# A loop over further token blocks, moved ahead of the experts behind eight weight loads

## The chip, the cores and the metric

The kernel runs on one core of a Trainium2 chip. The metric is the time on the device, in microseconds (us), of one execution; each kernel is run several times and the median is given. The core's engines run side by side and wait for each other by semaphores: PE is TensorE (matrix products and transposes through the identity), DVE is VectorE, ACT is ScalarE, POOL is GpSimd, and SP is SyncE, which here only issues the large loads. Each engine carries out its own instructions in a fixed order.

## The reference

Two model blocks, one after the other, over 1024 tokens of width 1024, in float32. The first has two token mixers and a feed-forward part; the second has two more mixers and a mixture of experts. Only the last is touched by the change:

```python
p_group = softmax(h @ wg + bg)            # 4 groups
pg, g_sel = top_k(p_group, 1)
e_in = (h @ we + be)[the 8 experts of g_sel]
top_v, top_i = top_k(e_in, 2)
gates = softmax(top_v) * pg
ids = g_sel * 8 + top_i                   # 2 of 32 experts for each token
hg = xs @ w_gate[e];  hu = xs @ w_up[e]   # [1024] -> [512], rows xs of expert e
y  = (silu(hg) * hu) @ w_down[e]          # [512] -> [1024]
out = rmsnorm(x + sum over both of gate * y)
```

A token goes to two experts, so 2048 rows are shared out over 32 experts. How many an expert gets depends on the data; the kernel has to be right for any share.

## The kernel before, in words

**Products.** Each float32 matrix is split into a high part (a copy on ScalarE, line 56, `split`) and a low part (source minus high, line 57), which together are one "unit" of 128 x 1024 elements. The low part is VectorE's; among the experts every sixth (`self.nsplit % 6 == 5`) is GpSimd's. A product (`mm3`, lines 87 to 89) is three matmuls: high by high, high by low, low by high. The pool of units holds five.

**Weights.** They arrive in pieces of 1 MB in a ring of 14 slots (`rawt`); SP issues the loads in program order, each as soon as its slot is free.

**Routing** (`route`). It makes for each expert the list of its rows: the first 128 of each expert come straight into a table on the chip (`self.sidx` and `self.slots`), and all of them are also written as records to a list in memory, `lst`, by eight indirect DMAs on GpSimd for each half of the tokens (`scatter`, line 1255). The scatter of the second half is kept as `self.scatter` and called among the experts, at `e == 2`.

**Experts** (`stage5`, from line 1269). For each of 32 experts one block of 128 rows is processed. `gather(e)` fetches the rows by an indirect DMA on GpSimd into one of two tiles xg (line 1298). `prep(e)` transposes them on TensorE; ScalarE and VectorE evict the result as xT (line 138). `wide` makes gate and up products (tile gu), 4 units each; a tanh on ScalarE (th, line 1357) and two VectorE operations make the hidden values; `hidT` transposes them (hT, line 138); `down` makes the product dn from 4 units. Its two halves are scaled by the gate while ScalarE evicts them as y (line 1338), and an indirect DMA scatters the rows to `yd` (line 1339). The loop is staggered by one: turn e makes the gate product of expert e, then the transposes of the hidden values of e−1, the up product of e, the transposes of the input of e+1, and the down product of e−1. A turn has 12 units, 72 matmul products of 512 columns and 12 transposes; two of its units have a low part by GpSimd.

**Further blocks** (`overflow`, from line 1387). For an expert with more than 128 rows a loop whose count is known only on the chip processes the remaining blocks. TensorE sums the counts (line 1396, `cnt`), VectorE makes from them a table of blocks (lines 1399 to 1417), each engine loads the number of blocks into a register (line 1418), and all five engines enter the loop at line 1420; its body reads `lst`. It is called at `e == NX // 2`, that is, behind 16 of 32 experts.

**Order.** The program is written in one stream, and a scheduler decides the order on each engine from its dependences and estimated times. It doesn't move instructions across the loop at line 1420. So what stands ahead of the loop, its body, and what stands behind it are ordered apart.

**End.** Behind the experts the two rows of each token are added, normed and written out (lines 1371 to 1385).

Of the kernel before, what the change touches and what calls it, by code (L numbers as in the profile page):

```python
# [8 lines left out]
F32 = mybir.dt.float32  # L9
# [7 lines left out]
P = 128  # L17
S = 1024
D = 1024
# [5 lines left out]
NX = NG * NE  # L25
DE = 512
BIG = 1 << 20
OFF = 4096
# [3 lines left out]
class Net:  # L32
# [27 lines left out]
    def t_units(self, w, cols):  # L60
        """Column tiles (128 wide) of w [K, N]; loaded in pairs where they adjoin."""
        nc = self.nc
        i = 0
        while i < len(cols):
            c = cols[i]
            n = 2 if i + 1 < len(cols) and cols[i + 1] == c + P else 1
            raw = self.raw_p.tile([P, KD, n * P], F32, tag="raw", name="raw")
            nc.sync.dma_start(raw, w[:, c:c + n * P].rearrange("(k p) c -> p k c", p=P))
            for j in range(n):
                yield self.split(raw[:, :, j * P:(j + 1) * P], [KD, P])  # L70
            i += n

    def n_units(self, w, r0, nk, c0):
        """Row tiles of w, 512 columns from c0, two row tiles a unit."""
        nc = self.nc
        for k in range(0, nk, 4):
            m = min(4, nk - k)
            raw = self.raw_p.tile([P, m, 512], F32, tag="raw", name="raw")
            nc.sync.dma_start(
                raw, w[r0 + k * P:r0 + (k + m) * P, c0:c0 + 512].rearrange("(k p) c -> p k c", p=P))  # L80
            for j in range(0, m, 2):
                yield k + j, self.split(raw[:, j:j + 2], [2, 512])

    def mm3(self, out, w, x, first, last):
        """out += w^T x, both as (high, low) pairs; w is the one held in the array."""
# [5 lines left out]
    def col(self, ps, unit, xT, n0=0, n=HT):  # L91
        """ps [128 columns, n tokens] = unit^T xT"""
# [7 lines left out]
    def pair(self, slot, name):  # L100
        """A (high, low) pair [128, 8, 512] in one of the two large slots."""
# [8 lines left out]
    def rstd(self, pool, ssq, n, scale=1.0):  # L110
        """(scale * ssq / n + eps) ^ -0.5 for [128, m]"""
        nc = self.nc
# [7 lines left out]
    def norm(self, pool, x, gB, out):  # L120
        """out = rmsnorm(x) * g for a natural tile [128, 1024]"""
# [7 lines left out]
    def to_T(self, psp, xn, dst, t0, nk=KD, k0=0, tag="tp"):  # L129
        """dst (high, low) [:, k, t0:t0+128] = xn[:, k*128:(k+1)*128]^T"""  # L130
# [10 lines left out]
    def rows_T(self, psp, wk, tmp, specs, name, tag="tp"):  # L141
        """Vectors of DRAM, as rows of 128, turned to columns: {name: [128, n] AP}."""
# [17 lines left out]
    def stage1(self):  # L160
        tc, nc, a = self.tc, self.nc, self.a
        self.x2d = self.dram.tile([S, D], F32, name="x2d")
        with ExitStack() as ctx:
# [56 lines left out]
            # softplus(-lambda)  # L220
# [6 lines left out]
            # block-diagonal maps of the heads 2c, 2c + 1 for c of a pair  # L227
# [12 lines left out]
            for hf in range(2):  # L240
                T0 = hf * HT

                # short convolution branch
# [42 lines left out]
                # recurrent branch  # L286
                yb = self.pair(1 - hf, "yb")
                for c in range(0, 8, 2):
# [25 lines left out]
                    def gates():  # L314
                        for j in range(2):
# [7 lines left out]
                            # x = -log a = 4 sp (1 + tr);  1 - a = (1 + e^-x) tanh(x / 2)  # L323
# [7 lines left out]
                        # sqrt(1 - a^2) = (1 + a) sqrt(tanh(x / 2))  # L331
# [36 lines left out]
                # the next transposed input is made while the last product runs  # L368
# [23 lines left out]
    def put(self, dst, k, src):  # L392
        """dst (high, low) [:, k] = src"""
# [4 lines left out]
    def softplus(self, tmp, out, x, sgn, bias=0.0):  # L398
        """out = log(1 + exp(y)), y = sgn * x + bias; tmp() gives a tile like out."""
# [5 lines left out]
        # log1p(e) = 2 atanh(z), z = e / (2 + e) <= 1/3  # L405
# [11 lines left out]
    def stage2(self):  # L417
        tc, nc, a = self.tc, self.nc, self.a
        with ExitStack() as ctx:
# [78 lines left out]
            # the last two pairs by halves, so that the next input is ready in time  # L498
# [18 lines left out]
    def stage4(self):  # L517
# [11 lines left out]
        with ExitStack() as ctx:  # L529
# [38 lines left out]
            # the router's norm weight goes into its matrix  # L568
# [5 lines left out]
            # rows 0..15: dt of the heads, 32..39: i, 64..71: f  # L574
# [42 lines left out]
            def half(hf, xT, box):  # L617

# [27 lines left out]
                # dt rows halved, since xs is held doubled  # L646
# [18 lines left out]
                # exponents: decay | wc;  exp(acs) | inter;  - | exp(-m)  # L665
# [20 lines left out]
                # natural columns: [token, chunk, (16 heads | 8 heads)]  # L686
# [16 lines left out]
                def conv_silu(u, cw, cb, halo, i, n, out):  # L703
                    """out = 2 silu(conv(x) + b) for channel tile i of n"""
# [132 lines left out]
                def out_row(yT, q, u):  # L837
                    """The product of one row tile of w_out, token tile by token tile."""
# [44 lines left out]
                def heads(p, R):  # L883
                    """The two heads of a pair, each in three parts: weights, chunks, result."""
# [31 lines left out]
                    def part_c(e):  # L916
# [23 lines left out]
                        # h = num / den, normed over its 128 channels  # L940
# [8 lines left out]
                        # the weights of the state are spent: their place takes the result  # L949
# [18 lines left out]
                def mix_M(p, R, late):  # L968
                    """Two heads; between their parts stands what is left of the two before."""
# [41 lines left out]
            for hf in range(2):  # L1011
# [7 lines left out]
                for kind, j, n in units:  # L1019
# [14 lines left out]
                    if hf and kind == "M" and j < 3:  # L1034
                        # the routing of the first half stands between the heads of the second
# [11 lines left out]
    def merge(ga, na, gb, nb):  # L1047
        """The steps of ga with nb steps of gb spread among them."""
# [8 lines left out]
    def weave(self, ga, na, gb, nb):  # L1057
        """Traces the steps of two generators in turn."""
# [19 lines left out]
    def route_const(self):  # L1078
# [8 lines left out]
        # descending ranks, for the first of equals  # L1087
# [18 lines left out]
    def route(self, hf, src, wk, small, wide, mx):  # L1106
        """Experts, gates and places of half the tokens, in steps; their records go to the experts' lists."""
# [4 lines left out]
        for tt in range(4):  # L1112
            x = src(tt)
            t = hf * 4 + tt
            # the logits come from x itself: its norm's scale follows, its weight is in the matrix
# [17 lines left out]
        # 0 .. 127 along the row; low[q, p] = 1 where q < p; ones  # L1133
# [22 lines left out]
        def first_max(x, n, top, one):  # L1156
            """top = max of x [P, 4, n], one = one-hot of its first place"""
# [27 lines left out]
        # gates: softmax of the two, times the group's probability; halved for the doubled silu  # L1185
# [13 lines left out]
        # places: those before in the tile, in the tiles before and in the half before  # L1199
# [12 lines left out]
        n = 0  # L1212
        qs = []
        for s, gt in ((0, pg), (1, m2)):
# [7 lines left out]
            # what a slot of an expert's first block holds: row of the result, token, gate;  # L1222
            # less OFF, so that slots without a token stand out of bounds
# [18 lines left out]
        for s, r, gt in ((0, r1, pg), (1, r2, m2)):  # L1242
            # row of the list = pos * 32 + 8 * group + expert, both as 4 - rank and 8 - rank
# [25 lines left out]
    def stage5(self):  # L1269
        tc, nc, a = self.tc, self.nc, self.a  # L1270
        self.wctx.close()
        with ExitStack() as ctx:
# [34 lines left out]

            def wide(w, e, xT):
                ps = psa.tile([P, DE], F32, tag="gu", name="gu", bufs=4)
                for k in range(0, KD, 4):  # L1310
                    raw = self.rawt([P, 4, DE])
                    nc.sync.dma_start(raw, w[e, k * P:(k + 4) * P, :].rearrange("(k p) c -> p k c", p=P))
# [12 lines left out]
            def down(e, hT):  # L1325
                pd = [psa.tile([P, 512], F32, tag="dn", name="dn") for _ in range(2)]
                for k in range(0, 4, 2):
                    raw = self.rawt([P, 2, D])
                    nc.sync.dma_start(raw, wd[e, k * P:(k + 2) * P, :].rearrange("(k p) c -> p k c", p=P))
# [16 lines left out]
            self.ysc = []  # L1346
            gather(0)
            gather(1)
            xT = prep(0)
            prev = None  # L1350
            for e in range(NX + 1):
# [14 lines left out]
                if e == 2:  # L1366
                    self.scatter()
                if e == NX // 2:
                    # the other tile of xg holds the next but one
                    self.overflow(mid, wk, psa, xg[(e + 1) % 2])  # L1370
# [16 lines left out]
    def overflow(self, mid, wk, psa, x):  # L1387
        """Blocks of 128 tokens past an expert's first, as many as there are."""
# [31 lines left out]
        with tc.For_i(0, nb) as i:  # L1420
            e = nc.sync.value_load(ti[0:1, bass.ds(i, 1)], min_val=0, max_val=NX - 1)
# [123 lines left out]
```

## Time and profile before

| | us |
|---|---|
| median of three runs | 3396.74 |
| the three runs | 3396.74, 3402.04, 3393.51 |
| the profiled execution, its span | 3397.5 |
| span less median | 0.8 |

| engine | busy us | share of the span |
|---|---|---|
| PE | 3230.0 | 95% |
| DVE | 2072.2 | 61% |
| ACT | 1419.9 | 42% |
| POOL | 609.1 | 18% |

The profile records one execution; the trace's zero is the start of the span. The experts begin at about 2716 us with the gather of the first rows and end at 3345.5; the 52 us behind that are the end of the kernel. A row of a timeline gives start, duration, engine, line, operation, output<-input, how many alike stand together, and in brackets the idle time of the engine before it and what released it. Neighbouring products overlap in the records: of two products that start 0.23 us apart each may show 0.40. [...]

### The profile page before, as it was taken

The numbers are of one execution on the slowest core, as the hardware profiler recorded it, in microseconds if no ns is written. First come the engines' busy times: TensorE is split into PE (matmuls) and PEld (weight loads), VectorE is DVE, ScalarE is ACT, GpSimd is POOL, SyncE is SP. The second block draws the span as 40 slices with busy tenths as digits, with TensorE's granted clock in tenths as the row PEclk, the third lists the DMA queues.
The fourth block names the chain that finished last, engine by engine and source line by source line (L and its number), as shares of the span: only waits on it lengthen the run. The fifth ranks groups of instructions, "written<-read, shape, count | busy, mean of one in ns | idle before, by whom it ended". The sixth has DMA issues, their size and how long they took to land. (4 is left out here: it accounts for less than half of the span.)

```text
span 3397.5 us, 39631 instructions
## 1 busy us (share of the span) xinstructions
PE 3230.0 (95%) x15457; PEld 2661.3 (78%) x15457; DVE 2072.2 (61%) x2869; ACT 1419.9 (42%) x1954; POOL 609.1 (18%) x649
## 2 busy tenths in 40 slices
PE   8999999999999999999999999899999899999993
PEld 6887888877778888888777888777888778878772
DVE  5437544365544334333787665877656678888886
ACT  3227432255321111111343333443443378878873
POOL 0002210011210000000232111132112143334433
PEclk9999999999999999999999999999999899999996
DMA  4332433323431111111323323243332699969993
GB/s 154 99 100 85 145 118 99 99 85 117 136 118 50 50 50 38 62 50 35 105 88 106 103 91 92 73 145 109 103 109 93 230 322 384 381 256 389 368 349 155
DMA packets 313080, 487.81 MB, mean 144 GB/s; under 512 B 28400, under 2 KB 190460, under 8 KB 311868
## 3 DMA queue, kind: packets, MB, share of 16 engines
q1 hardware_dynamic: 291532, 427.02, 36.5%
q0 software_dynamic: 19488, 51.44, 4.2%
q10 hardware_dynamic: 1872, 6.82, 0.5%
q8 instruction: 122, 2.00, 0.2%
q14 instruction: 66, 0.54, 0.0%
HBM read 465.65 MB, written 36.34 MB: 148 GB/s over the span
## 5 line engine op out<-in xcount | busy, mean ns | idle before, releaser
L57 DVE TENSOR_TENSOR unit<-raw,unit 128x1024 fp32r<-128x1024 f32 x682 | 887.0, 1321 | 434.1 <-ACT unit L56 427.1
L56 ACT ACTIVATE unit<-raw 128x1024 fp32r<-128x1024 f32 x746 | 775.8, 1057 | 770.7 <-PE acc L89 689.5
L87 PE MATMUL acc<-xT,unit 128*128 128x512 f32 x1712 | 679.3, 397 | 0.1
L88 PE MATMUL acc<-xT,unit 128*128 128x512 f32 x1712 | 672.2, 393 | 0.0
L89 PE MATMUL acc<-xT,unit 128*128 128x512 f32 x1712 | 670.3, 392 | 0.0
L87 PEld LDWEIGHTS acc<-xT,unit 128*128 128x128 f32 x1712 | 323.7, 189 | 68.7 <-issue 1.2
L88 PEld LDWEIGHTS acc<-xT,unit 128*128 128x128 f32 x1712 | 323.4, 189 | 68.4 <-issue 3.6
L89 PEld LDWEIGHTS acc<-xT,unit 128*128 128x128 f32 x1712 | 323.2, 189 | 68.2 <-issue 1.0
L88 PE MATMUL gu<-unit,xT 128*128 128x512 f32 x512 | 207.3, 405 | 16.7 <-POOL unit L57 9.5
L87 PE MATMUL gu<-unit,xT 128*128 128x512 f32 x512 | 207.2, 405 | 1.1 <-ACT xT L138 0.8
L89 PE MATMUL gu<-unit,xT 128*128 128x512 f32 x512 | 204.5, 400 | 0.0
L88 PE MATMUL acc<-unit,xT 128*128 128x256 f32 (+1 forms) x640 | 196.4, 307 | 2.0 <-DVE unit L57 2.0
L87 PE MATMUL acc<-unit,xT 128*128 128x256 f32 (+1 forms) x640 | 193.9, 308 | 3.1 <-ACT xb L709 3.0
L89 PE MATMUL acc<-unit,xT 128*128 128x256 f32 (+1 forms) x640 | 195.4, 306 | 0.0
L57 POOL TENSOR_TENSOR unit<-raw,unit 128x1024 fp32r<-128x1024 f32 x64 | 157.7, 2464 | 156.8 <-issue 89.9
L482 DVE SCALAR_TENSOR_TENSOR xh<-acc,xh 128x512 f32<-128x512 f32 x160 | 110.4, 690 | 85.1 <-PE acc L89 84.5
L87 PE MATMUL acc<-unit,hid 128*128 128x512 f32 x352 | 137.3, 390 | 0.0
L89 PE MATMUL acc<-unit,hid 128*128 128x512 f32 x352 | 137.2, 390 | 0.0
L87 PE MATMUL acc<-x2T,unit 128*128 128x512 f32 x352 | 137.1, 389 | 0.1
L88 PE MATMUL acc<-unit,hid 128*128 128x512 f32 x352 | 137.1, 389 | 0.0
L88 PE MATMUL acc<-x2T,unit 128*128 128x512 f32 x352 | 136.9, 389 | 0.0
L89 PE MATMUL acc<-x2T,unit 128*128 128x512 f32 x352 | 136.9, 389 | 0.0
(425 smaller groups left out, 5641.0 us busy)
## 6 DMA issues: line engine op xcount, KB each, us to landing
raw<-in_w_in_dram SPq DMA_DIRECT2D x104, 1024.0 KB
raw<-in_exp_w_gate_dram SPq DMA_DIRECT2D x64, 1024.0 KB
raw<-in_exp_w_up_dram SPq DMA_DIRECT2D x64, 1024.0 KB
raw<-in_exp_w_down_dram SPq DMA_DIRECT2D x64, 1024.0 KB
raw<-in_w_ffn_gate_dram SPq DMA_DIRECT2D x11, 1024.0 KB
raw<-in_w_ffn_up_dram SPq DMA_DIRECT2D x11, 1024.0 KB
raw<-in_w_ffn_down_dram SPq DMA_DIRECT2D x11, 1024.0 KB
raw<-in_w_out_dram SPq DMA_DIRECT2D x9, 1024.0 KB
```

What stands on the lines that cost most here:

```text
L56: nc.scalar.activation(h, src, AF.Copy)
L57: (low or nc.vector).tensor_tensor(l, src, h.bitcast(F32), ALU.subtract)
L87: mm(out, w[0], x[0], start=first, stop=False)
L88: mm(out, w[0], x[1], start=False, stop=False)
L89: mm(out, w[1], x[0], start=False, stop=last)
L482: nc.vector.scalar_tensor_tensor(xs, ps, 0.5, xs, op0=ALU.mult, op1=ALU.add)
```

## The change

Eight weight loads are issued first: gate and up of expert 0, gate of expert 1, down of expert 0. The gathers of experts 0 and 1 follow, then the loop over further blocks, and behind it all experts; the four lines that fetched a piece of weights inside `wide` and `down` first look among those loaded ahead. The call of the loop at `e == NX // 2` and that of `self.scatter()` at `e == 2` are gone. The scatter now stands inside the loop's body: it is carried out once for each turn of the loop, and not at all when there is none. The loop gets a tile of its own for its rows (`xo`), cleared in the body. Comments were removed as well; those lines are left out here.

```diff
+            ahead = {}
+            def wload(w, e, k):
+                raw = self.rawt([P, 4, DE])
+                nc.sync.dma_start(raw, w[e, k * P:(k + 4) * P, :].rearrange("(k p) c -> p k c", p=P))
+                return raw
+            def dload(e, k):
+                raw = self.rawt([P, 2, D])
+                nc.sync.dma_start(raw, wd[e, k * P:(k + 2) * P, :].rearrange("(k p) c -> p k c", p=P))
+                return raw
             def wide(w, e, xT):
                 ps = psa.tile([P, DE], F32, tag="gu", name="gu", bufs=4)
                 for k in range(0, KD, 4):
-                    raw = self.rawt([P, 4, DE])
-                    nc.sync.dma_start(raw, w[e, k * P:(k + 4) * P, :].rearrange("(k p) c -> p k c", p=P))
+                    raw = ahead.pop((w is wu, e, k), None)
+                    if raw is None:
+                        raw = wload(w, e, k)
...
                 for k in range(0, 4, 2):
-                    raw = self.rawt([P, 2, D])
-                    nc.sync.dma_start(raw, wd[e, k * P:(k + 2) * P, :].rearrange("(k p) c -> p k c", p=P))
+                    raw = ahead.pop((2, e, k), None)
+                    if raw is None:
+                        raw = dload(e, k)
...
             self.ysc = []
+            for key in ((0, 0, 0), (0, 0, 4), (1, 0, 0), (1, 0, 4), (0, 1, 0), (0, 1, 4), (2, 0, 0), (2, 0, 2)):
+                j, e, k = key
+                ahead[key] = dload(e, k) if j == 2 else wload((wg, wu)[j], e, k)
             gather(0)
             gather(1)
+            self.overflow(mid, wk, psa, mid.tile([P, D], F32, tag="gB", name="xo"))
+            self.nraw = len(ahead)
             xT = prep(0)
...
                 if e:
                     down(e - 1, hT)
-                if e == 2:
-                    self.scatter()
-                if e == NX // 2:
-                    self.overflow(mid, wk, psa, xg[(e + 1) % 2])
                 prev, xT = th, nxt
...
         with tc.For_i(0, nb) as i:
+            self.scatter()
+            nc.gpsimd.memset(x, 0.0)
             e = nc.sync.value_load(ti[0:1, bass.ds(i, 1)], min_val=0, max_val=NX - 1)
```

How the change moves instructions is seen best at two places. The first is GpSimd at the start of the experts, from the clearing of the two tiles of gathered rows on. Before, the gathers are followed by a unit's low part and the records (line 1255), and the loop's ones (ov_22097) come behind them:

```order
L1291 MEMSET xg_19399 128x1024
L1291 MEMSET xg_19400 128x1024
L1298 DMA xg_19399<-h2d,sidx 128x1024
L1298 DMA xg_19400<-h2d,sidx 128x1024
L57 TENSOR_TENSOR unit<-raw,unit 128x1024
L1255 DMA lst<-rec,row 32768x4 x4
L1298 DMA xg_19399<-h2d,sidx 128x1024
L1255 DMA lst<-rec,row 32768x4 x3
L1394 MEMSET ov_22097 128x128
L1405 IOTA ov_i 128x16
```

And the same place now (ov_19427 are the ones that the counts are summed with, ov_t is the table with the number of blocks; the row of line 1255 is in the loop's body):

```order
L1291 MEMSET xg_19399 128x1024
L1291 MEMSET xg_19400 128x1024
L1298 DMA xg_19399<-h2d,sidx 128x1024
L1298 DMA xg_19400<-h2d,sidx 128x1024
L1410 MEMSET ov_19427 128x128
L1421 IOTA ov_i 128x16
L1434 TENSOR_LOAD ov_t
L1436 COMPARE_AND_BRANCH
L1436 ISA
L1436 UNCONDITIONAL_BRANCH
L1436 ISA
L1255 DMA lst<-rec,row 32768x4 x8
```

What moved: the ones for the counts stand directly behind the two gathers, the loop's entry follows, and the low part of the first unit and the records have gone behind the entry.

The second place is ScalarE in one turn some twelve experts ahead of the end. Before, the copies (line 56) run in groups of five, three and four, and both halves of y stand together:

```order
L138 ACTIVATE hT_23019<-tp 128x512
L56 ACTIVATE unit<-raw 128x1024 x5
L138 ACTIVATE xT_23069<-tp 128x512 x2
L56 ACTIVATE unit<-raw 128x1024 x3
L1338 ACTIVATE y_23126<-dn,slots 128x512 x2
L56 ACTIVATE unit<-raw 128x1024 x4
L1357 ACTIVATE th_23176<-gu 128x512
```

And the same turn now:

```order
L138 ACTIVATE hT_23021<-tp 128x512
L56 ACTIVATE unit<-raw 128x1024 x2
L138 ACTIVATE xT_23071<-tp 128x512 x2
L56 ACTIVATE unit<-raw 128x1024 x2
L1378 ACTIVATE th_23018<-gu 128x512
L56 ACTIVATE unit<-raw 128x1024 x7
L1352 ACTIVATE y_23128<-dn,slots 128x512
L56 ACTIVATE unit<-raw 128x1024
L1352 ACTIVATE y_23128<-dn,slots 128x512
```

What moved: the tanh stands between the fourth and the fifth copy of the turn, and a copy stands between the halves of y. Before, too, ScalarE leaves its steady order towards the end; there a turn reads:

```order
L138 ACTIVATE hT_24456<-tp 128x512
L56 ACTIVATE unit<-raw 128x1024
L1338 ACTIVATE y_24406<-dn,slots 128x512 x2
L56 ACTIVATE unit<-raw 128x1024
L138 ACTIVATE xT_24506<-tp 128x512
L56 ACTIVATE unit<-raw 128x1024 x2
L138 ACTIVATE xT_24506<-tp 128x512
L56 ACTIVATE unit<-raw 128x1024 x2
L1357 ACTIVATE th_24453<-gu 128x512
L56 ACTIVATE unit<-raw 128x1024 x6
```

In the kernel before, an order unlike the steady one stands for the last 408 of the experts' 2304 products; in the changed kernel for the last 1056.

## Rows read from the trace of the kernel before

**Rows 1.** The page: busy engines, and the costliest groups of instructions.
```profile
PE 3230.0 (95%) x15457; PEld 2661.3 (78%) x15457; DVE 2072.2 (61%) x2869; ACT 1419.9 (42%) x1954; POOL 609.1 (18%) x649
...
L57 DVE TENSOR_TENSOR unit<-raw,unit 128x1024 fp32r<-128x1024 f32 x682 | 887.0, 1321 | 434.1 <-ACT unit L56 427.1
...
L88 PE MATMUL gu<-unit,xT 128*128 128x512 f32 x512 | 207.3, 405 | 16.7 <-POOL unit L57 9.5
...
L57 POOL TENSOR_TENSOR unit<-raw,unit 128x1024 fp32r<-128x1024 f32 x64 | 157.7, 2464 | 156.8 <-issue 89.9
```
**Rows 2.** Windows: stretch and length, busy us by engine, clock, DMA share, GB/s.
```profile
core 0: us, PE busy (x) PEld busy (x) DVE busy (x) ACT busy (x) POOL busy (x), PEclk, DMA share, GB/s
...
2756.02:3027.77 271.75, 271.75 (x1263) 220.94 (x1262) 237.40 (x227) 232.34 (x270) 109.66 (x60) 1.00 0.96 357
3027.77:3076.07 48.30, 39.28 (x173) 30.55 (x171) 39.89 (x49) 30.97 (x36) 16.88 (x8) 0.93 0.78 294
...
3202.80:3222.95 20.15, 18.70 (x86) 14.35 (x84) 17.53 (x15) 13.21 (x16) 7.89 (x4) 1.00 1.01 365
3222.95:3243.60 20.65, 20.29 (x97) 15.99 (x96) 15.96 (x17) 16.11 (x21) 8.43 (x5) 1.00 1.02 381
...
3285.60:3308.50 22.90, 20.36 (x86) 15.71 (x85) 17.45 (x15) 14.91 (x18) 5.80 (x3) 0.93 0.86 305
3308.50:3329.80 21.30, 18.18 (x77) 13.68 (x77) 16.64 (x14) 13.94 (x16) 5.80 (x3) 1.00 0.14 53
3329.80:3345.50 15.70, 13.66 (x52) 10.01 (x50) 9.77 (x8) 6.33 (x8) 3.37 (x2) 0.89 0.03 12
```
**Rows 3.** Timeline of TensorE around the loop.
```profile
3034.09 0.30 PE L1396 MATMUL cnt<-cum,ov 128*128 128x32 f32 x2
3041.36 1.12 PE L135 MATMUL tp<-ident,th 128*128 128x128 f32 x4 [6.97 <-DVEq L1420]
3042.45 0.79 PE L87 MATMUL gu<-unit,xT 128*128 128x512 f32 x1
```
**Rows 4.** Timeline of VectorE around the loop.
```profile
3034.42 0.19 DVE L1399 COPY ov_n<-cnt 128x32 f32<-128x32 f32 x1 [3.90 <-PE cnt L1396]
...
3042.74 1.23 DVE L57 TENSOR_TENSOR unit<-raw,unit 128x1024 fp32r<-128x1024 f32 x1 [2.69 <-PE tp L135]
```
**Rows 5.** Timeline of TensorE at the start of the experts.
```profile
2722.49 1.97 PE L135 MATMUL tp<-ident,xg 128*128 128x128 f32 x8 [5.79 <-DMA xg<-h2d,sidx]
...
2742.49 0.79 PE L88 MATMUL gu<-unit,xT 128*128 128x512 f32 x1 [2.77 <-DVE unit L57]
```
**Rows 6.** Timeline of GpSimd at the start of the experts.
```profile
2719.61 1.89 POOL L1298 DMA_INDIRECT xg<-h2d,sidx  x1 [0.31 <-issue]
...
2724.14 1.04 POOL L1255 DMA_INDIRECT lst<-rec,row  x1 [0.17 <-issue]
```
**Rows 7.** Line 1298, the gathers: from issue to landing.
```profile
DMA to landing us min/median/max: 4.3/7.2/8.2
```
**Rows 8.** Timeline of ScalarE in the turn from 3308.50.
```profile
3313.87 1.39 ACT L1338 ACTIVATE y<-dn,slots 128x512 f32<-128x512 f32 x2 [1.49 <-PE dn L89]
3315.15 4.83 ACT L56 ACTIVATE unit<-raw 128x1024 fp32r<-128x1024 f32 x5
3323.22 0.60 ACT L1357 ACTIVATE th<-gu 128x512 f32<-128x512 f32 x1 [3.23 <-PE gu L89]
```
**Rows 9.** Timeline of GpSimd in that turn.
```profile
3316.53 2.38 POOL L57 TENSOR_TENSOR unit<-raw,unit 128x1024 fp32r<-128x1024 f32 x1
3325.84 2.43 POOL L57 TENSOR_TENSOR unit<-raw,unit 128x1024 fp32r<-128x1024 f32 x1 [6.94 <-ACT unit L56]
```
**Rows 10.** Timeline of TensorE in the last turns.
```profile
3297.46 0.63 PE L87 MATMUL gu<-unit,xT 128*128 128x512 f32 x1
3297.88 0.63 PE L88 MATMUL gu<-unit,xT 128*128 128x512 f32 x1
...
3318.96 0.50 PE L88 MATMUL gu<-unit,xT 128*128 128x512 f32 x1 [2.21 <-POOL unit L57]
```
**Rows 11.** Timeline of VectorE in that turn.
```profile
3326.69 2.67 DVE L57 TENSOR_TENSOR unit<-raw,unit 128x1024 fp32r<-128x1024 f32 x1 [0.67 <-ACT unit L56]
```

## The prediction

> **What bounds the kernel now.** I read the page's busy table first. TensorE is busy for 95% of the span and every other engine for 61% or less [rows 1], so time can only come from TensorE's waits, its half clock, or the order in which it is fed. The change touches the experts alone, so I cut them into stretches with the window view [rows 2]. The reader is to see three prices there. Fifteen turns of the expert loop take 271.75 us with TensorE busy throughout: 18.1 us a turn. The 48.30 us around the loop over further blocks hold the work of two turns (36.2), so the loop costs 12.1. And from 3202.80 on turns are dearer although nothing was added to them: 20.15 in the first window, then 20.65, later 22.90 and 21.30.
>
> Two timelines explain the first two prices. At the loop TensorE ends its count product, VectorE turns the counts into a block count, and everything stands until 3041.36, idle for 6.97 [rows 3, 4]; then transposes and a product run at half clock. No instruction inside the loop shows in the trace, and the gate products on line 88 number 512, which is 32 experts by 16 [rows 1]: on this data the loop makes no turn, and its price is its entry. At the start TensorE idles 5.79 until the first gathered rows land [rows 5].
>
> The third price is an order. In the steady part ScalarE makes high halves well ahead of TensorE; in the last turns it stands behind the evictions y and the tanh th, which need TensorE's newest results, and the unit that TensorE needs next is split behind them. Every sixth low half is GpSimd's, at 2.46 us instead of VectorE's 1.32 [rows 1]. In the turn from 3308.50, y ends at 3315.26, the split follows, GpSimd works from 3316.53 for 2.38, and TensorE, idle for 2.21, goes on at 3318.96 [rows 8 to 10]. The last 408 expert products, 5.67 turns, took from 3222.95 to 3345.50 in this order [rows 2], which is 122.55 us where 102.6 (5.67 by 18.1) were due: a loss of 20, 3.5 a turn. It is not the weights: at 3308 the DMA share is 0.14 and the turn still takes 21.3 [rows 2].
>
> **The change, part by part.**
>
> *The loop leaves the middle.* The 12.1 us of [rows 2] go. What is late next there: nothing new, since the turns on both sides run at 18.1 with the same code. −12.1.
>
> *The loop stands at the start.* Its entry is then paid where TensorE waits for the gather anyway. The count product needs ones that GpSimd sets, and that memset now stands behind both gathers, the second of which is issued by 2721.50 [rows 6]. From there 7.27 us, the distance from the count product to the first instruction behind the loop in [rows 3], give about 2728.4 for TensorE's first transpose; before it was 2722.49 [rows 5]. That is +6. Five splits on ScalarE and four on VectorE, done in that wait until now, come behind the loop, and VectorE resumes 1.38 after TensorE (3042.74 against 3041.36 [rows 3, 4]), so the first products wait some 2 more. The stall of 2.77 at 2742.49 [rows 5] shrinks by perhaps 0.7. Sum +7.5. From below, if the memset goes ahead and the landing hides the entry, +4; from above, if the entry on GpSimd waits for the gathers to land (4.3 to 8.2 us [rows 7]) and not only for their issue, +12. I take 7.5, since [rows 3] is the same loop.
>
> [...]
>
> *Eight loads go ahead of the loop; six more follow it.* Before, all 14 slots of the ring were loaded in the wait. A turn needs six loads of 1 MB, and the queue moves 357 GB/s in the steady turns and up to 381 in the late ones [rows 2], so eight loads are over a turn's head start: nothing, up to +3 if it starves once.
>
> *The later records move into the loop.* Seven of their eight indirect DMAs on GpSimd ran beside expert 0, off TensorE's path, about 1 us each [rows 6]; as the loop makes no turn, they never run. GpSimd's own splits come earlier by that: 0 to −0.7, counted above.
>
> *The loop divides the program for the scheduler.* This is the large term. In the order of the changed kernel ScalarE keeps the steady pattern for some 18 turns, then falls into a late one for the last 1056 products, 14.67 turns: nine more than before. The pattern is new: transposed hidden values, two splits, two evictions of xT, two splits, tanh, seven splits, half of y, a split, the other half. GpSimd's two splits in a turn are the second behind the tanh and the one between the halves of y, both on a circle that closes on TensorE. Along it, with durations of [rows 8 to 10]: tanh 0.7 with its hand-over, two splits 2.0, GpSimd 2.4, and 0.75 as the middle of what a VectorE operation in progress adds; the rest of that unit on TensorE 1.2 (five products, starting 0.233 apart in the steady part); three units of down products, two transposes and hand-over 5.6; half of y 0.7; split 1.06; GpSimd 2.4; rest of the unit 1.2; two units and four transposes 3.25. Sum 21.3, a loss x of 3.2 a turn. Measured late turns bound it from above at 22.90 − 18.1 = 4.8 and from below at 2.05 (20.15 − 18.1) [rows 2]; if the new pattern hid GpSimd altogether, 0. So this term is 14.67 by 3.2 less the 20 lost before: 47 − 20 = +27.
>
> On the 0.75: VectorE's split at 3326.69 took 2.67 instead of the mean 1.32, ending 1.1 us after GpSimd's at 3325.84 had ended [rows 1, 9, 11]. [...]
>
> *Sum.* −12.1 + 7.5 + 14.67x − 20 = 14.67x − 24.6. At x = 3.2 that is +22.3. On the profiled span of 3397.5 it makes 3419.8; the median of the runs shown, 3396.74, is 0.8 lower, so 3419.
>
> **Rivals.**
>
> *The new late order costs little (faster).* Each half of y is 0.7 and the split stands between them, so GpSimd starts 0.7 sooner than in [rows 8, 9]; if TensorE has a whole unit more in hand at that point, both GpSimd splits are hidden. The point from which it decides is x = 1.7, where the sum is zero. At x = 0.5 the sum is −17: 3380. For it: seven splits stand together behind the tanh. Against it: the pool of units holds five, so ScalarE cannot run far ahead, and every late turn measured lost 2 or more. Chance 6%.
>
> *Both terms cancel (same).* With x between 1.0 and 2.4 the result is within 10 us of before; x = 2.05, the cheapest turn measured, gives +5.5: 3402. Chance 12%.
>
> *The clock falls too.* In the turn from 3285.60, the granted clock is 0.93: after a wait, products start 0.42 apart, from 3297.46 on [rows 10], and the turn is 1.6 us dearer than the next listed [rows 2]. If each of the 14.67 turns lost about 1.5, +22 more: 3441. Against it: of the four whole late turns listed only this one is below 1.00. Chance 8%.
>
> *The entry waits for the gathers to land.* +12 for the start instead of 7.5: 3424. It lies inside the forecast's own spread, with 15% of the chance.
>
> That the change does nothing is excluded by the order; that the loop body runs would need counts above 128, which the 512 products exclude.
>
> **How the numbers follow.** The forecast with x from 2.4 to 4.0 holds 59%, and with the late entry 15% and the falling clock 8% the slower side is 82%. Within 0.3% (10 us, what a measurement of this kernel can tell from no change) is 12%, faster 6%. x = 2.0 gives about 3401 and x = 4.2 about 3434; leaving a tenth out on either side, the range is 3400 to 3434.
>
> **What would show it.** Right: TensorE without a stop at about 3030; a first transpose near 2728; turns of 18.1 until some 15 are left, then about 21, with idle time of line 88 released by GpSimd's split rising from 9.5 [rows 1] to some 30. Wrong: late turns at 19 or less, a start more than 12 us late, or TensorE waiting for weights.

## The result, and the profile after

| | before | after |
|---|---|---|
| median of four runs, us | 3396.49 | 3418.32 |
| lowest and highest | 3393.51, 3402.04 | 3415.45, 3421.03 |
| span of the profiled execution | 3397.5 | 3413.5 |

The ratio is 1.006, with a 95% interval from 1.0046 to 1.0075: slower by 22 us. The forecast was 3419.

The spans differ by 16.0 only. Up to the last routing product ahead of the experts, which the change doesn't touch, the profiled execution of after is 4.4 us ahead (line 1233 starts at 2708.60 instead of 2713.01), and the difference builds up in stretches at half clock that stand in one execution and not in the other. The largest stands in before from 2529.34 to 2536.17 at a granted clock of 0.50, with products 0.43 apart; the same products of after, from 2526.5 on, run at 1.00 and 0.23 apart, and after gains 3.1 there. So I count from that product's start on, to the start of the experts' last product plus one spacing of 0.23 (the ends of products are modelled): 632.6 us before and 653.5 after, +21.0; the end of the kernel gives back 0.5.

The page of after, the lines that answer to [rows 1]. The wait of the gate and up products for GpSimd's low halves went from 9.5 to 25.2 us:

```profile
PE 3229.4 (95%) x15457; PEld 2652.1 (78%) x15457; DVE 2081.7 (61%) x2869; ACT 1415.4 (41%) x1954; POOL 614.0 (18%) x641
...
L88 PE MATMUL gu<-unit,xT 128*128 128x512 f32 x512 | 211.7, 413 | 32.5 <-POOL unit L57 25.2
L57 POOL TENSOR_TENSOR unit<-raw,unit 128x1024 fp32r<-128x1024 f32 x64 | 166.6, 2602 | 253.7 <-ACT unit L56 192.6
```

The windows of after, to be read against [rows 2] (columns as there). The stretches are cut at products, so that each holds whole turns: 14, one, one, one, 11, one, and the last.

```profile
2769.15:3022.64 253.49, 253.49 (x1180) 206.42 (x1178) 221.29 (x210) 216.88 (x253) 102.82 (x57) 1.00 1.02 384
3022.64:3041.41 18.77, 18.36 (x87) 14.66 (x86) 15.42 (x14) 13.14 (x17) 7.35 (x4) 1.00 1.03 375
3041.41:3060.81 19.40, 18.80 (x87) 14.42 (x86) 15.75 (x15) 14.76 (x18) 8.30 (x4) 1.00 1.02 372
3060.81:3081.98 21.17, 19.60 (x95) 15.45 (x93) 15.60 (x17) 16.25 (x21) 8.64 (x5) 1.00 1.03 376
3081.98:3318.49 236.51, 210.81 (x925) 158.30 (x924) 188.61 (x166) 164.09 (x199) 91.72 (x42) 1.00 0.90 314
3318.49:3339.53 21.04, 18.30 (x78) 13.56 (x77) 17.66 (x16) 13.95 (x17) 7.46 (x3) 1.00 0.42 153
3339.53:3362.14 22.61, 19.96 (x77) 14.57 (x75) 14.73 (x12) 12.71 (x15) 5.80 (x3) 0.92 0.02 8
```

The 14 turns take 18.11 each and TensorE never stops. The 11 take 21.50 each at full clock; nothing stands at 3030 any more. TensorE's timeline at the start, against [rows 5]:

```profile
2716.32 0.63 PE L1412 MATMUL cnt<-cum,ov 128*128 128x32 f32 x2 [4.02 <-POOL ov L1410]
2724.67 1.97 PE L135 MATMUL tp<-ident,xg 128*128 128x128 f32 x8 [7.72 <-issue]
...
2728.45 0.79 PE L89 MATMUL gu<-unit,xT 128*128 128x512 f32 x1 [0.54 <-DVE xT L139]
```

One late turn of after, from 3146.48 to 3168.02: ScalarE (columns as in [rows 8]), then GpSimd, then TensorE's waits in it. The split at 3159.89 stands between the halves of y, GpSimd's low half of it runs from 3161.07 to 3163.46, and TensorE goes on at 3163.51. GpSimd's other split, 3149.31, starts beside one of VectorE's and takes 3.33; TensorE waits for it at 3152.70. The last row of ScalarE is the tanh of the next turn.

```profile
3146.68 0.60 ACT L1378 ACTIVATE th<-gu 128x512 f32<-128x512 f32 x1
3147.17 5.80 ACT L56 ACTIVATE unit<-raw 128x1024 fp32r<-128x1024 f32 x6
3154.22 1.06 ACT L56 ACTIVATE unit<-raw 128x1024 fp32r<-128x1024 f32 x1 [1.25 <-PE gu L89]
3159.30 0.69 ACT L1352 ACTIVATE y<-dn,slots 128x512 f32<-128x512 f32 x1 [4.02 <-PE dn L89]
3159.89 1.05 ACT L56 ACTIVATE unit<-raw 128x1024 fp32r<-128x1024 f32 x1
3160.83 0.68 ACT L1352 ACTIVATE y<-dn,slots 128x512 f32<-128x512 f32 x1
...
3168.21 0.60 ACT L1378 ACTIVATE th<-gu 128x512 f32<-128x512 f32 x1
```
```profile
3149.31 3.33 POOL L57 TENSOR_TENSOR unit<-raw,unit 128x1024 fp32r<-128x1024 f32 x1 [3.94 <-ACT unit L56]
3161.07 2.39 POOL L57 TENSOR_TENSOR unit<-raw,unit 128x1024 fp32r<-128x1024 f32 x1 [8.43 <-ACT unit L56]
```
```profile
3150.44 0.50 PE L88 MATMUL gu<-unit,xT 128*128 128x512 f32 x1 [0.41 <-DVE unit L57]
3152.70 0.50 PE L88 MATMUL gu<-unit,xT 128*128 128x512 f32 x1 [0.59 <-POOL unit L57]
...
3163.51 0.50 PE L88 MATMUL gu<-unit,xT 128*128 128x512 f32 x1 [1.26 <-POOL unit L57]
```

### The profile page after: what moved, and what is told of

It reads as the page before. It is cut to its first block, busy times and chain, and to the rows that moved or that the text cites. A ratio compares the mean times of both kernels' runs of the same rounds, so it can differ in the third digit from the quotient of the medians.

```text
span 3413.5 us, 39624 instructions
## 1 busy us (share of the span) xinstructions
PE 3229.4 (95%) x15457; PEld 2652.1 (78%) x15457; DVE 2081.7 (61%) x2869; ACT 1415.4 (41%) x1954; POOL 614.0 (18%) x641
## 5 line engine op out<-in xcount | busy, mean ns | idle before, releaser
L88 PE MATMUL gu<-unit,xT 128*128 128x512 f32 x512 | 211.7, 413 | 32.5 <-POOL unit L57 25.2
L57 POOL TENSOR_TENSOR unit<-raw,unit 128x1024 fp32r<-128x1024 f32 x64 | 166.6, 2602 | 253.7 <-ACT unit L56 192.6
L88 PEld LDWEIGHTS gu<-unit,xT 128*128 128x128 f32 x512 | 96.9, 189 | 75.9 <-POOL unit L57 37.9
L87 PE MATMUL acc<-x2T,unit 128*128 128x512 f32 x352 | 137.1, 389 | 0.1
L88 PE MATMUL acc<-x2T,unit 128*128 128x512 f32 x352 | 136.9, 389 | 0.0
```

Source lines behind the costliest of these rows:

```text
L57: (low or nc.vector).tensor_tensor(l, src, h.bitcast(F32), ALU.subtract)
L87: mm(out, w[0], x[0], start=first, stop=False)
L88: mm(out, w[0], x[1], start=False, stop=False)
```

## The experiments

Counting the rows of ScalarE's order gave the theory its final form. In the steady turns ScalarE has made, whenever it comes to a tanh, hT or y, the splits of **four units beyond** the one whose product that eviction waits for. In the late turns, in both kernels, it has made two at the tanh and one at y. So in the steady part TensorE has four units in hand while ScalarE waits for it, in the late part one or two, and those may be GpSimd's. Theory 1: the lead, and GpSimd's slow split inside it, cost the 3.4 us a turn. All totals below are medians in us; the kernel before, run beside them, had medians of 3397.35 to 3398.05.

**e1: all low halves on VectorE**, ScalarE's late order unchanged.

```diff
-                return self.split(src, shape, low=nc.gpsimd if self.nsplit % 6 == 5 else None)
+                return self.split(src, shape, low=None)
```

> The changed kernel with all low halves of the experts on VectorE, none on GpSimd; ScalarE's order keeps the same late pattern over the last 15 turns. Theory 1 (GpSimd's slow split, twice a turn, lies on the circle that closes on TensorE): the two pieces of 2.4 + 0.75 become 1.3 each, 3.7 us less a turn; VectorE's own load (12 splits of 1.3 and some 4 us of other work, 19.6) then bounds the turn: late turns at 18.8 to 19.8 instead of 21.5, clean turns up from 18.1 to at most 19.6; total 3390 to 3425. Rival 2 (the order on ScalarE by itself costs, whichever engine makes the low half): late turns stay at 21 or more, total 3415 or more.

3385.17, ratio to before 0.9961 (0.9948 to 0.9975). Its late turns take 19.39, inside theory 1's range. The total lies below the 3390 to 3425 expected: the clean turns take 18.11 still, where up to 19.6 had been allowed for. VectorE is busy for 182.55 of 210 us, so its load as a whole doesn't set the late turn either; the short waits that TensorE has left name VectorE's splits. Window and waits of e1 (waits: who waited for whom, us, times, longest):

```profile
3090.00:3300.00 210.00, 205.56 (x912) 157.03 (x911) 182.55 (x185) 161.03 (x196) 28.57 (x20) 1.00 1.00 356
```
```profile
PE gu L88 <- DVE unit L57: 4.4, 11, 0.4
```

Of the 3.4 us of a late turn 2.1 go with GpSimd's splits and 1.3 stay: GpSimd is most of the price, not all. How much of the 2.1 is GpSimd's slower split and how much what the two engines cost each other (e4, e8), this run doesn't tell. The kernel is 33 us faster than after by a change that makes the busiest helper, VectorE, busier.

**e2: the early hT and xT undone.** Each of these evictions is kept behind what is written ahead of it on ScalarE.

```diff
-            nc.scalar.activation(h, ps, AF.Copy)
+            i = nc.scalar.activation(h, ps, AF.Copy)
+            if pin:
+                pin(i)                      # tc.keep_in_program_order
...
-                    nc.scalar.activation(th, pg, AF.Tanh, scale=0.5)
+                    tc.keep_in_program_order(nc.scalar.activation(th, pg, AF.Tanh, scale=0.5))
```

> The changed kernel with the evictions hT, xT, th and y kept in program order on ScalarE. This undoes the early transposes of the late pattern, but ScalarE is still only one or two units ahead of TensorE at th and y, instead of four in the steady turns. If the lead is what counts (theory 1, completed): late turns stay at 20.5 to 22, total 3405 to 3425. If the place of hT and xT ahead of th is what costs (rival 3): late turns at 18.1 to 19, total 3370 to 3385.

3413.9, late turns 20.75: theory 1's side. The place of hT and xT is worth 0.75 a turn; the rest goes with the lead, which at tanh and y is two and one in this kernel too.

**e3: the lead itself.** A generator hands out units, and the splits are written four ahead of their use; the pins of e2 keep the evictions there.

```diff
+            todo, made = stream(), []
+            def unit():
+                while len(made) < 4 + 1:
+                    made.append(next(todo, None))
+                return made.pop(0)
...
-                        u = split(raw[:, j:j + 2], [2, DE])
+                        u = unit()
```

> The changed kernel with the units' splits written four ahead of their use, and the evictions kept in that order, so that ScalarE is four units ahead at every tanh, hT and y in all turns; loop, loads and records as in the changed kernel. Theory 1: every turn at 18.1; the 1.95 and 14 times 3.4 us of the late turns go, 3418 less 49.6 is 3368 to 3370. Rival 4 (late turns cost because of something late in the run, as weights or the clock): late turns stay near 21, total above 3405.

3373.67, ratio 0.9926 (0.9912 to 0.994). The turns from the 20th on take 18.09; three on the way there take 18.6 to 18.8, and the last one, in which the work runs out, 21.4. All four were reckoned at 18.1; that is some 5 us, and the total missed 3370 by 3.7. In the place where after has its late turns TensorE doesn't wait once:

```profile
3080.00:3297.00 217.00, 217.00 (x1009) 176.89 (x1008) 190.77 (x181) 184.41 (x217) 95.67 (x46) 1.00 1.00 372
```

The loads and the place in the run are the same, the clock is 1.00 in both, and the weights come faster, at 372 GB/s where after moved 314: rival 4 falls, and the late price was order.

**e8: a lead of three** in the last 15 turns (`3 + 1` in the loop above).

> The run e3_lead4 with the splits written three units ahead instead of four; the first 16 turns have four all the same, the 15 behind them three. Theory: each unit ahead is 1.4 us of TensorE's work on either side of the circle; with one or two ahead a turn took 21.5 or 20.8, so with three 18.1 to 18.9, total 3373 to 3387. Rival (any lead under the whole pool stalls on GpSimd's split alike): turns at 20 or more, total 3400 or more.

3397.16, turns of 20.13: the rival's side, though its total, 3400, was missed by 3. One unit less than four costs 2.0 a turn, one or two more less (e2) only another 0.6. The 1.4 us for each unit was wrong, and with it the picture in which every unit of lead buys its own length. The waits of e8 in its late turns name VectorE; its window shows VectorE busy for 234.44 of 261 us. GpSimd, VectorE and TensorE in one turn show why:

```profile
PE gu L88 <- DVE unit L57: 19.3, 14, 1.8
```
```profile
3061.00:3322.00 261.00, 241.34 (x1088) 189.23 (x1087) 234.44 (x195) 195.44 (x234) 101.72 (x50) 1.00 0.93 327
```
```profile
3152.34 3.29 POOL L57 TENSOR_TENSOR unit<-raw,unit 128x1024 fp32r<-128x1024 f32 x1 [2.11 <-issue]
```
```profile
3153.32 3.39 DVE L57 TENSOR_TENSOR unit<-raw,unit 128x1024 fp32r<-128x1024 f32 x1
```
```profile
3156.77 0.50 PE L88 MATMUL gu<-unit,xT 128*128 128x512 f32 x1 [1.35 <-DVE unit L57]
```

GpSimd's split runs until 3155.63. VectorE's, which starts inside it, takes 3.39 and ends 1.08 behind it; the splits of VectorE ahead of it and behind it take 1.21 each. TensorE goes on at that end. So with a lead of three TensorE waits for a VectorE split that ends only behind GpSimd's.

**e4: the records alone.**

```diff
-                if e == 2:
-                    self.scatter()
...
         with tc.For_i(0, nb) as i:
+            self.scatter()
```

> The kernel before with one part of the change: the eight later indirect DMAs of records stand in the loop's body (never run on this data), the loop stays in the middle. ScalarE's order is the same as before throughout. Theory: they ran beside expert 0 off TensorE's path, so 0 to -0.7 us, no difference that can be measured. Rival 5 (they delay GpSimd's first splits and gathers on the path): -2 to -4 us.

3397.73, ratio 0.9993 (0.9984 to 1.0003): by time, neither. The trace says more. VectorE's splits in the turn of expert 0 and the split of GpSimd beside them, first in before (where TensorE's wait behind them is the 2.77 of [rows 5]); then the same in e4, with TensorE's wait:

```profile
2733.13 1.22 DVE L57 TENSOR_TENSOR unit<-raw,unit 128x1024 fp32r<-128x1024 f32 x1
2735.45 4.12 DVE L57 TENSOR_TENSOR unit<-raw,unit 128x1024 fp32r<-128x1024 f32 x1 [1.09 <-ACT unit L56]
```
```profile
2736.06 2.42 POOL L57 TENSOR_TENSOR unit<-raw,unit 128x1024 fp32r<-128x1024 f32 x1
```
```profile
2741.07 2.27 DVE L57 TENSOR_TENSOR unit<-raw,unit 128x1024 fp32r<-128x1024 f32 x1 [1.09 <-ACT unit L56]
```
```profile
2739.76 2.50 POOL L57 TENSOR_TENSOR unit<-raw,unit 128x1024 fp32r<-128x1024 f32 x1 [8.47 <-ACT unit L56]
```
```profile
2746.26 0.50 PE L88 MATMUL gu<-unit,xT 128*128 128x512 f32 x1 [0.93 <-DVE unit L57]
```

The first turn falls from 25.7 to 23.4. So the records were not off the path. In both kernels VectorE's split ends 1.09 or 1.08 behind GpSimd's; but behind the records GpSimd's split came late, after VectorE's had started, and VectorE's took 4.12 instead of 2.27. (Why VectorE's, begun 0.6 earlier, didn't end first is not shown.) The issues of the records by themselves did not slow it: the split at 2733.13, with two of them beside it (from 2732.24 for 1.07 and from 2733.61 for 1.57), took 1.22.

**e5: the loop back in the middle**, with e3's lead on both sides of it (not across).

> The kernel before (loop behind 16 experts, records among the experts) with the splits written four units ahead, as in the run e3_lead4, but not across the loop. Theory: the late turns of before go (about 18 us with the turn before them) and the 12.1 of the loop in the middle stays: 3378 to 3382. Then the loop ahead of the experts is by itself worth 5 to 8 us (3373.7 with the same order). Rival: the order in the middle was what the loop's place bought, and the two kernels come out alike, within 3 us of 3373.7.

3383.92, ratio 0.9958 (0.9944 to 0.9971), against e3's 3373.67: the theory's side, with a total 2 above its range. Counted from the last routing product to the experts' end as above, 615.5 against 608.1: with the order held, the rest of the change is a **gain of 7.4**. That is the loop's place, the loads ahead and the records together; the records' part is the 2.3 of e4's first turn.

**e6: no loop at all.**

> The run e3_lead4 without the loop over further blocks at all (its counts, its entry and its body are left out; on this data it makes no turn). Theory: TensorE's first transpose stands 9.5 us behind the last routing product's start instead of 16.07, so -5 to -7 us against 3373.7: 3367 to 3369. Rival (the entry is hidden behind the landing of the gather): within 2 us of 3373.7.

3351.17: the direction of the theory, but 16 us below it. The start is as forecast, 9.53 from the last routing product to the first transpose, where e3 has 16.08 (6.5 us). The rest is something else: its clean turns take 17.69 instead of 18.11, with the same work in each.

**e9 and e10: the layout.** Leaving the loop out also removes its tiles, and what lies behind them moves, xT and hT among it, from which TensorE loads its weights here. Both runs change one width:

```diff
-        ti = mid.tile([P, 2 * NB + 1], I32, name="ov_t")
+        ti = mid.tile([P, 48], I32, name="ov_t")
```

> The run e3_lead4 with one tile of the loop's preparation, the table ov_t, made 192 bytes wide for each partition instead of 132, so that the tiles behind it (xT and hT, from which TensorE loads its weights among the experts) start on a multiple of 64 bytes, as they did in e6_lead4_no_loop, and not 32 off it. Theory: that layout, not the loop's absence, made e6's products start 0.227 apart instead of 0.234 and its turns 17.69 instead of 18.11; 30 turns by 0.42 is -13: 3360 to 3362. Rival (the loop in the program costs that, as by a semaphore or the code): turns stay at 18.11, total 3373.

> The kernel before with nothing changed but that width of ov_t (192 bytes instead of 132). Theory: its 23 turns of 18.11 fall to 17.69, the late ones, which wait, by less: -9 to -13, total 3385 to 3389. Rival: nothing, 3397.

e10: 3383.15, ratio 0.996 (0.9944 to 0.9975), clean turns 17.69: the layout makes the difference, and a little more of it than expected. e9: 3374.74, 18.13: a multiple of 64 is not what counts. Windows of before, e10 and e9, 240 us each in clean turns; TensorE's count is what to compare:

```profile
2770.00:3010.00 240.00, 240.00 (x1116) 195.09 (x1115) 209.41 (x200) 205.00 (x239) 94.63 (x53) 1.00 0.97 362
```
```profile
2770.00:3010.00 240.00, 240.00 (x1140) 199.89 (x1139) 214.51 (x203) 210.43 (x245) 99.33 (x55) 1.00 0.99 366
```
```profile
2790.00:3030.00 240.00, 240.00 (x1113) 195.09 (x1112) 209.55 (x200) 205.27 (x240) 95.91 (x53) 1.00 1.02 383
```

**e7: the ones first.**

> The run e3_lead4 with the ones for the counts set ahead of the clearing of the gathered rows, so that the count product needs not wait for GpSimd's two gathers. Theory (the entry's length counts from the count product): the first transpose 4 us earlier, 12 instead of 16.07 behind the last routing product's start; total 3369 to 3371. Rival (the entry waits for the gathers to land): the first transpose moves by less than 1 us, total 3373.

3371.55; the first transpose moved from 16.08 to 15.45. The rival. The block numbers (line 1421, an iota) had stayed behind the gathers, so VectorE's chain began late too; but it ended at 2725.48, and TensorE went on 4.2 us later, where before it was 1.3. GpSimd was last. At the loop's entry it carries out a step of 2.01 us (INC_SWDGE_SEM), and ahead of it it waited 3.82. Its rows at the entry (durations in ns: least, median, longest; then first and last start), and the time from issue to landing of the two gathers (least, median, longest):

```profile
L1455 POOLq EVENT_SEMAPHORE  x17: 17/43/3819, 2721.9 to 2729.6; - x17
L1455 POOLq INC_SWDGE_SEM  x1: 2007/2007/2007, 2726.1 to 2726.1; - x1
```
```profile
DMA to landing us min/median/max: 4.4/4.8/5.3
```

The second gather was issued at 2720.67 and landed 5.3 later, at 2725.94; the step started at 2726.10 and ended at 2728.11; TensorE went on at 2729.69.

**e11: one gather ahead of the loop,** ones and block numbers first.

```diff
             gather(0)
-            gather(1)
-            self.overflow(mid, wk, psa, mid.tile([P, D], F32, tag="gB", name="xo"))
+            self.overflow(mid, wk, psa, xg[1], ones, io)
+            gather(1)
```

> The run e9_lead4_aligned with the ones and the block numbers of the counts set ahead of the clearing of the gathered rows, and with only the first gather ahead of the loop (the loop's rows go to the second tile xg, so that the second gather comes behind it; the last norm's weight, which could take its place there, is loaded at the start of the experts). Theory, as e7 left it: the entry waits for the transfers that GpSimd issued ahead of it to land; with one gather left, first transpose 11.5 to 13.5 us behind the last routing product's start instead of 16.07: total -2.5 to -4.5 against e9. Rival (counts and barrier set it whatever the gathers do, or the second gather is then late for expert 1): no gain, or a stall before expert 1.

The first transpose comes at 13.09, as expected, 3 us earlier than with two gathers, and there is no stall before expert 1. GpSimd's step starts at 2726.47, half a us behind the last packet of the one gather (2725.95), and TensorE goes on 1.58 behind the step's end, as in e7. By time nothing can be told: 3374.46, runs from 3365.22 to 3379.01.

**e12: a tile of the mixers widened** (`sib`, 64 bytes instead of 4), on e11.

> The run e11_entry_one_gather with a tile of the second block's mixers (sib) 64 bytes wide instead of 4, which puts the weights of the 768 output products (yT) and of the small products there on multiples of 64 bytes too. Theory: their spacing falls from 0.234 to 0.227: 768 by 0.007 is 5.4, some more for the small ones: -4 to -8 against e11. Rival: they lie beside other work and nothing is seen, 0 to -2.

3368.6, the lowest median here that keeps the loop: ratio to before 0.9912 (0.9894 to 0.993), and 5.9 below e11. The output products went from 0.2341 apart to 0.2326 only, 1.2 us for 768 of them; where the rest comes from is not settled, since e11's runs spread over 14 us. A version that has e3's lead, e11's entry and the layout of e10 wasn't run.

## Why the prediction was right, point by point

**−12.1 for the loop in the middle: right.** The two turns there take 38.17 instead of the 48.30 of [rows 2]; the 1.95 above twice 18.11 belongs to the late order, which begins there.

**+7.5 for the start: right in the first part, too dear in the second.** The first transpose comes 16.07 us behind the last routing product's start instead of 9.48: +6.6, where +6 was worked out (2721.50 and 7.27 make 2728.8 and +6.3; the 2728.4 is a slip). In after the entry took 8.35 from the count product on, and the count product came 0.8 earlier than reckoned. But by the end of the second turn only 5.1 are left. The products' first wait was 0.54 (2728.45 above) and not 2, and the records that no longer run give back 2.3 in the first turn by e4. Their cost, "0 to −0.7", was mis-sized.

**What sets the entry: the forecast's chain, level with a step that it didn't know.** The forecast took the count chain of [rows 3]; the rival had the entry wait for the gathers to land. In after both gathers had landed by then: the second was issued at 2715.03 and took 4.8. GpSimd had its number of blocks at 2720.48, its step at the entry started at 2721.11 without a long wait, and it ended at 2723.12. VectorE's chain ended at 2722.74, and its load of the number of blocks at 2723.12 too. The gathers' landing, GpSimd's step, and VectorE's load (columns as in e7):

```profile
DMA to landing us min/median/max: 4.0/4.4/4.8
```
```profile
L1436 POOLq INC_SWDGE_SEM  x1: 2007/2007/2007, 2721.1 to 2721.1; - x1
```
```profile
L1434 DVEq TENSOR_LOAD <-ov_t x1: 546/546/546, 2722.6 to 2722.6; - x1
```

So the rival's wait is real, as e7 and e11 show, but it didn't set the time of this change: it comes to light when the counts are done earlier. That GpSimd's step and the counts ended together is chance, and it is why the number worked out from the counts alone held.

**+27 for the late turns: right, and decisive.** From the turn at 3022.64 on, the experts lose 49.7 us against turns of 18.11; before it was 33.9 from the same turn on, 12.1 of it the loop's. 49.7 − 21.8 is +27.9. x was forecast as 3.2 and is 3.4; the wait for GpSimd's halves was forecast as some 30 and is 25.2. That order was the cause is shown by e3, which takes some 45 of the 49.7 away, and GpSimd's part by e1. Why the scheduler leaves its steady order where it does was not looked into.

**The circle behind x: right, term by term.** The rows of the late turn above can be followed round it. From the tanh at 3146.68 to GpSimd's split at 3149.31 it is 2.63 (forecast 2.7); that split takes 3.33 (3.15, with the 0.75); from its end to y at 3159.30 it is 6.66 (6.8); from y to GpSimd's second split at 3161.07 it is 1.77 (1.76); that one takes 2.39 (2.4); and from its end to the next tanh at 3168.21 it is 4.75 (4.45). The sum is 21.53, where 21.26 was forecast. The 0.75 was the author's estimate, the middle of a range, and no run shows it as such: in the 11 late turns the first of GpSimd's two splits starts with 1.06 to 1.08 left of one of VectorE's and takes 3.31 to 3.33, some 0.9 more than the second, which starts beside none and takes 2.36 to 2.39. What e8 refuted is the idea added later, that each unit of lead is worth 1.4 us: with another lead another circle closes, there through VectorE.

**Loads ahead: right.** No wait for weights shows in after, and the clean turns move 384 GB/s. **The falling clock: it didn't come.** The 11 late turns stand at 1.00; only the last window shows 0.92.

Sum by the trace: +5.1 − 12.1 + 27.9 = +20.9, less 0.5 at the end; the medians say +21.8, the forecast +22.3. The start was forecast 2.4 too dear and the late turns 0.9 too cheap, so the two errors offset in part.

## What to carry to other kernels

A scheduler's region is part of the cost of moving a loop: look at the order on the engine that feeds TensorE far behind the place of the change, and count how many results it holds ready at each point where it must wait for TensorE itself. If that lead falls, write the producer ahead of its use in the program, rather than leave it to priorities; here it was worth 45 us, more than all the rest of the change. And leave room in a count for what leaving out a part does to the layout: an experiment without the loop measured two things at once.

## What the runs showed of the hardware that was not expected

**The spacing of products went with the place of the weights.** The experts' products of 512 columns at full clock start 0.227 apart in some kernels and 0.233 in others, with the same work. The offset of the weights' tile in its partition, in bytes modulo 256 as the built program places it, against the mean spacing: 96 (before) 0.233; 128 (e10) 0.227; 160 (e3) 0.233; 128 (e6) 0.227; 192 (e9) 0.233; for the output products of the mixers 224 (all but e12) 0.234 and 0 (e12) 0.233. The moving operand is at 128 in all of them. The other large groups of such products in before, where both operands are at 128, start 0.227 to 0.228 apart. So the fast ones are those where both have the same offset; whether equality or the value 128 matters was not tried. In the experts it is 0.42 us a turn, and 14 us for the kernel before by one tile's width.

**At this loop's entry GpSimd's step comes behind the landing of its own transfers.** The step takes 2.01 us in after and e7 (0.73 in before). In e7 GpSimd waited 3.82 ahead of it, and it starts 0.16 behind the landing of the second gather; in e11 it starts half a us behind the last packet of its one gather. In after it runs from 2721.11 to 2723.12 beside the counts, which end at 2722.74, and is not added to them. TensorE goes on 1.3 to 1.6 us behind the later of the two: 1.3 behind the counts in before, 1.55 behind the step in after, 1.58 in e7 and e11.

**VectorE's split beside one of GpSimd's.** A split of VectorE that outlasts one of GpSimd's ends 1.08 to 1.14 us behind it, in all 63 cases among the experts of before, with starts from 0.61 ahead of GpSimd's start to 2.32 behind it, and takes from 1.22 to 4.12; alone it takes 1.21 to 1.23, and beside GpSimd's other work, issues of indirect DMAs above all, at most 1.27. So GpSimd's splits cost VectorE time even where nobody waits for GpSimd, as in e8 (3.39 where the splits ahead of it and behind it take 1.21), and its DMA issues do not: 1.27 at most against 1.23.

**On the order:** the section on the kernel says that the scheduler moves nothing across the loop. That holds for work that depends on what stands there. In before the load of the last norm's weight, written behind all experts, ran ahead of the loop (which stands at 3034), since it waits for nothing new:

```profile
2735.44 0.62 POOL L107 DMA_DIRECT2D gB<-in_norm_f_w_dram  x1
```

e11 guards against that by giving the loop the second gather's tile; the order without it wasn't run.
